# Rotary embedding on one core: VectorE one row ahead instead of two, the last rows without TensorE, and one semaphore less

## The chip, the cores and the metric

The kernel runs on one core of one Trainium2 chip. The metric is the device time of one execution in microseconds, the median of several. The profile's own clock runs from the first to the last instruction or landing, and is about 1.4 us shorter than the measured time (161.2 us in the profile of an execution of 162.6 us). Here a run counts as slow when it took over 1.5% more than the fastest of the same kernel.

## The reference

```python
# x: (16, 512, 1024) fp32, num_heads = 16, head_dim = 64; cos, sin: (512, 32)
x = x.reshape(batch, seq, num_heads, head_dim)
x1, x2 = x[..., :half_dim], x[..., half_dim:]
out = concatenate([x1 * cos - x2 * sin, x1 * sin + x2 * cos], axis=-1)   # fp32
```

33.5 MB come in and 33.5 MB go out. Each element takes two products and one sum.

## The kernel before

The 16 x 512 positions form 8 groups of 8 "rows". A row is a 128 x 1024 tile, a group 4 MB. SBUF and PSUM are the two memories on the chip in which the kernel keeps its tiles. The ring, a buffer in SBUF whose places are used again in turn, holds five groups. A semaphore is a counter that one engine or DMA raises and another engine waits for. For each row u:

- VectorE multiplies x by cos into one of three PSUM buffers, `t1_ps`.
- GpSimd multiplies the swapped halves of x by -sin and sin into one of six SBUF buffers, `t2_sb`. In row 3 of each group VectorE does this.
- The two are added, by VectorE (rows 0, 2, 4, 5, 7) or by TensorE with an identity matrix, after which ScalarE copies the sum out of PSUM (rows 1, 3, 6).
- When a whole group is added, ScalarE's queue issues its store. A load into a used place of the ring waits for the store of the group that was there. The first load and the last store are split into two halves of 2 MB.

```python
PE2 = [u % 8 in (1, 3, 6) for u in range(NU)]        # rows added by TensorE
V2 = [u % 8 == VROW for u in range(NU)]              # sine product by VectorE
NT1 = 3; NT2 = 6; LEAD = 2
# ... cut ...
            for u in range(NU):                      # on TensorE
                if not PE2[u]:
                    continue
                pe.wait_ge(sem_m, u + 1)
                if V2[u]:
                    pe.wait_ge(sem_d, n_dve[u])
                else:
                    pe.wait_ge(sem_p, n_pool[u])
# ... two matmuls with the identity, added to t1_ps ...
            def mul(u):                              # on VectorE
                # ... wait for the load when a new one begins ...
                if V2[u]:
                    wait_t2_free(ve, u)
                    ve.tensor_tensor(t2_sb[:, u % NT2, :, :, :], swapped(k), over_heads(s_ps), mult
                    ).then_inc(sem_d, 1)
                if u >= NT1:                         # the PSUM buffer of row u - 3 must be free
                    v = u - NT1
                    if PE2[v]:
                        ve.wait_ge(sem_a, n_pe[v])
                    else:
                        ve.wait_ge(sem_v, n_comb[v])
                ve.tensor_tensor(t1_ps[:, u % NT1, :] ..., x_sb[...], c_ps[...], mult).then_inc(sem_m, 1)

            def comb(u):
                ve.wait_ge(sem_m, u + 1)
                ve.wait_ge(sem_p, n_pool[u])
                ve.tensor_tensor(xs[:, k, :], t1_ps[...], t2_sb[...], add).then_inc(sem_v, 1)

            for u in range(NU + LEAD):
                if u < NU:
                    mul(u)
                if u >= LEAD and not PE2[u - LEAD]:
                    comb(u - LEAD)
```

## Time and profile before

| before | value |
|---|---|
| time, median of the first 3 runs | 162.17 us (162.09 to 162.74) |
| profiled span | 161.2 us |
| VectorE, GpSimd busy | 131.5, 130.2 us |
| moved by DMA | 67.39 MB |
| VectorE's longest waits | 9.3 us for ScalarE, in 6 places |

The view of the waits (engine, line, tile, what it waited for: total us, times, longest us) has for the kernel before:

```profile
DVE t_ps L247 <- ACT x_sb L161: 9.3, 6, 3.1
...
POOL t_sb L216 <- DMA x_sb<-in_x_dram: 7.5, 3, 3.5
```

And the chain that ended last, by line:

```profile
DVE x_sb L258 20%; PE t_ps L187 20%; DVE t_ps L247 15%; POOL t_sb L216 6%; ACT x_sb L161 5%; DMA stage<-in_sin_dram 4%; DVE t_sb L238 4%; SPq L142 0%; SPq L145 0%; ACT s_sb L154 0%; ACT s_sb L155 0%; DVEq L246 0%; DVEq L257 0%; DVEq L244 0%; POOLq L134 0%
```

Read alone, this chain says that compute sets the time, and it nearly leaves the DMA out. It follows the last instruction back, and the last instruction ends at 151.4 us. The program ends 9.8 us later, with a store.

### The profile page before, as it was taken

How to read it: one execution, taken by the hardware profiler on the slowest of the kernel's cores; microseconds unless marked ns; L12 is line 12 of the kernel's file. 1: busy time of each engine (PE TensorE's matmuls, PEld its weight loads, DVE VectorE, ACT ScalarE, POOL GpSimd, SP SyncE). 2: the span in 40 equal slices, each digit the busy share in tenths (PEclk: the TensorE clock that was granted, in tenths of full speed). 3: DMA queues.
4: the chain of work that ended last, by engine and by line, in shares of the span. 5: the costliest groups of instructions: out<-in, count | busy, mean ns of one | idle time of the engine just before them, and what ended most of it. 6: DMA issues, size and time to landing. Idle time of an engine off the chain costs nothing.

```text
span 161.2 us, 579 instructions
## 1 busy us (share of the span) xinstructions
PE 80.9 (50%) x102; PEld 24.8 (15%) x102; DVE 131.5 (82%) x116; ACT 26.6 (16%) x27; POOL 130.2 (81%) x62
## 2 busy tenths in 40 slices
PE   6002908249438434644844584494584483785000
PEld 1001302102202110120220121022022021211000
DVE  0079299998799999996999999996999899978500
ACT  3010221120221122202012202202202211211200
POOL 1049999999999999999999899973999659995000
PEclk9955796955585987655687659555558555558555
DMA  4999999999999999999999999999999999999995
GB/s 150 387 454 488 407 423 472 407 390 390 415 496 390 415 480 409 407 480 415 401 480 407 415 472 415 407 480 415 407 480 415 399 480 423 399 480 415 399 431 236
DMA packets 2882, 67.39 MB, mean 418 GB/s; under 512 B 320, under 2 KB 576, under 8 KB 576
## 3 DMA queue, kind: packets, MB, share of 16 engines
q1 hardware_dynamic: 1584, 33.82, 49.6%
q10 hardware_dynamic: 1296, 33.56, 48.3%
q14 instruction: 2, 0.02, 0.0%
HBM read 33.82 MB, written 33.55 MB: 418 GB/s over the span
## 4 chain that ended last, share of the span: by engine, by line
DVE 39%; PE 20%; issue 17%; POOL 6%; ACT 6%; DMA 4%; SPq 1%; DVEq 0%; POOLq 0%
DVE x_sb L258 20%; PE t_ps L187 20%; DVE t_ps L247 15%; POOL t_sb L216 6%; ACT x_sb L161 5%; DMA stage<-in_sin_dram 4%; DVE t_sb L238 4%; SPq L142 0%; SPq L145 0%; ACT s_sb L154 0%; ACT s_sb L155 0%; DVEq L246 0%; DVEq L257 0%; DVEq L244 0%; POOLq L134 0%
## 5 line engine op out<-in xcount | busy, mean ns | idle before, releaser
L216 POOL TENSOR_TENSOR t_sb<-x_sb,s_sb 128x1024 f32<-128x1024 f32 x56 | 129.5, 2369 | 16.2 <-ACT s_sb L155 8.8
L187 PE MATMUL t_ps<-t_sb,ident 128*128 128x512 f32 x96 | 78.2, 964 | 67.3 <-DVE t_ps L247 49.7
L247 DVE TENSOR_TENSOR t_ps<-x_sb,tab_ps 128x1024 f32<-128x1024 f32 x64 | 77.2, 1227 | 11.1 <-ACT x_sb L161 9.3
L258 DVE TENSOR_TENSOR x_sb<-t_ps,t_sb 128x1024 f32<-128x1024 f32 x40 | 48.6, 1218 | 0.0
L161 ACT ACTIVATE x_sb<-t_ps 128x1024 f32<-128x1024 f32 x24 | 24.6, 1024 | 115.9 <-PE t_ps L187 115.9
L187 PEld LDWEIGHTS t_ps<-t_sb,ident 128*128 128x128 f32 x96 | 24.0, 275 | 120.8 <-DVE t_ps L247 88.0
L238 DVE TENSOR_TENSOR t_sb<-x_sb,tab_ps 128x1024 f32<-128x1024 f32 x8 | 9.7, 1210 | 0.0
L225 DVE COPY tab_ps<-stage 128x256 f32<-128x256 f32 x1 | 0.4, 428 | 7.8 <-DMA stage<-in_cos_dram 7.8
L173 PE MATMUL t_ps<-zero 128*128 128x512 bf16 x6 | 2.7, 630 | 1.3 <-DVE zero L221 1.3
L154 ACT ACTIVATE s_sb<-stage 128x256 f32<-128x256 f32 x1 | 0.4, 416 | 7.2 <-DMA stage<-in_sin_dram 7.2
L154 ACT ACT_TABLE_LOAD x1 | 1.3, 1283 | 0.8 <-PEq L291 0.8
L173 PEld LDWEIGHTS t_ps<-zero 128*128 128x128 bf16 x6 | 0.7, 137 | 2.4 <-DVE zero L221 1.2
L221 DVE MEMSET zero<- 128x256 uint32 x1 | 0.3, 272 | 0.9 <-PEq L291 0.9
L198 POOL MEMSET ident<- 128x128 f32 x1 | 0.2, 204 | 0.3 <-POOLq L291 0.3
L155 ACT ACTIVATE s_sb<-stage 128x256 f32<-128x256 f32 x1 | 0.4, 399 | 0.0
L200 POOL TENSOR_SCALAR_AFFINE_SELECT ident<-ident 128x128 f32<-128x128 f32 x1 | 0.3, 292 | 0.1
L291 POOL MEMSET const-float32-0.0<- 128x1 f32 x1 | 0.1, 98 | 0.3 <-issue 0.3
L227 DVE TENSOR_SCALAR tab_ps<-stage 128x32 f32<-128x32 f32 x1 | 0.2, 195 | 0.0
L228 DVE COPY tab_ps<-stage 128x32 f32<-128x32 f32 x1 | 0.2, 184 | 0.0
L291 POOL MEMSET const-bfloat16-1.0<- 128x1 bf16 x1 | 0.1, 101 | 0.0
L291 POOL MEMSET const-uint8-127<- 128x1 uint8 x1 | 0.1, 101 | 0.0
L291 POOL MEMSET const-float32-1.0<- 128x1 f32 x1 | 0.1, 98 | 0.0
## 6 DMA issues: line engine op xcount, KB each, us to landing
x_sb<-in_x_dram SPq DMA_DIRECT2D x7, 4096.0 KB, 35.6
out_dram<-x_sb ACTq DMA_DIRECT2D x7, 4096.0 KB, 26.2
x_sb<-in_x_dram SPq DMA_DIRECT2D x2, 2048.0 KB, 9.6
out_dram<-x_sb ACTq DMA_DIRECT2D x2, 2048.0 KB, 10.2
stage<-in_cos_dram SPq DMA_DIRECT2D x1, 128.0 KB, 7.5
stage<-in_sin_dram SPq DMA_DIRECT2D x1, 128.0 KB, 7.2
```

Of the source, the lines that this page charges most:

```text
L154: ae.activation(s_sb[:, :, 0, :], sv, COPY, scale=-1.0)
L155: ae.activation(s_sb[:, :, 1, :], sv, COPY).then_inc(sem_s, 1)
L161: ae.activation(xs[:, k, :], t1_ps[:, u % NT1, :], COPY).then_inc(sem_a, 1)
L173: pe.matmul(t1_ps[:, k, b * BANK:(b + 1) * BANK], zero[:, 0:P], zero[:], start=True, stop=True).then_inc(sem_w, 1)
L187: ins = pe.matmul(t1_ps[:, u % NT1, b * BANK:(b + 1) * BANK], ident[:], t2[:, b * BANK:(b + 1) * BANK], start=False, stop=True, skip_group ...
L200: pl.affine_select(out=ident[:], in_=ident[:], compare_op=mybir.AluOpType.is_equal, fill=0.0, base=0, pattern=[[-1, P]], channel_multiplier=1,
L216: pl.tensor_tensor(t2_sb[:, u % NT2, :, :, :], swapped(k), over_heads(s_sb[:, r]), mult).then_inc(sem_p, 1)
L225: ve.tensor_copy(c_ps, cv)
L238: ve.tensor_tensor(t2_sb[:, u % NT2, :, :, :], swapped(k), over_heads(s_ps), mult).then_inc(sem_d, 1)
L247: ve.tensor_tensor(t1_ps[:, u % NT1, :].rearrange("p (h d) -> p h d", d=HALF), x_sb[:, k, :, :, :].rearrange("p h t d -> p (h t) d"), c_ps ...
L258: ve.tensor_tensor(xs[:, k, :], t1_ps[:, u % NT1, :], t2_sb[:, u % NT2, :, :, :].rearrange("p h t d -> p (h t d)"), add,).then_inc(sem_v, 1)
L291: nc = _bacc.Bacc("TRN2", target_bir_lowering=False, num_devices=1)
```

## The change

The intent: with a lead of two rows, VectorE's product u reuses the PSUM buffer that the sum just ahead of it has read, and must wait for that sum to finish. With a lead of one, that sum lies two instructions back. The last four rows are all added by VectorE, so that no detour over TensorE and ScalarE ends the kernel. The semaphore of VectorE's sine products goes: the cosine product of the same row comes after it in order and has a semaphore that TensorE waits for anyway.

```diff
-    PE2 = [u % 8 in (1, 3, 6) for u in range(NU)]
-    V2 = [u % 8 == VROW for u in range(NU)]
+    PE2 = [u < NU - R // 2 and u % 8 in (1, 3, 6) for u in range(NU)]
+    V2 = [u < NU - R // 2 and u % 8 == VROW for u in range(NU)]
...
-    LEAD = 2
+    LEAD = 1
...
-                if V2[u]:
-                    pe.wait_ge(sem_d, n_dve[u])
-                else:
+
+                if not V2[u]:
                     pe.wait_ge(sem_p, n_pool[u])
...
-                    ve.tensor_tensor(
-                        t2_sb[:, u % NT2, :, :, :], swapped(k), over_heads(s_ps), mult
-                    ).then_inc(sem_d, 1)
+                    ve.tensor_tensor(t2_sb[:, u % NT2, :, :, :], swapped(k), over_heads(s_ps), mult)
```

Of rows 60 to 63 only row 62 was on TensorE, so one sum moves to VectorE.

More of the change, by code (lines that the diff above doesn't have):

```diff
@@ L65, in bass_split_heads_rope_kernel @@
     n_pool = count([not v for v in V2])
-    n_dve = count(V2)
     n_pe = count(PE2)
@@ L95, in bass_split_heads_rope_kernel @@
         sem_p = stack.enter_context(nc.semaphore("pool"))
-        sem_d = stack.enter_context(nc.semaphore("dve2"))
         sem_m = stack.enter_context(nc.semaphore("mul"))
```

## The prediction

> **What bounds the kernel now.** I read the page first: engines, slices, DMA queues.
>
> ```profile
> PE 80.9 (50%) x102; PEld 24.8 (15%) x102; DVE 131.5 (82%) x116; ACT 26.6 (16%) x27; POOL 130.2 (81%) x62
> ...
> DMA  4999999999999999999999999999999999999995
> ...
> q1 hardware_dynamic: 1584, 33.82, 49.6%
> q10 hardware_dynamic: 1296, 33.56, 48.3%
> ...
> HBM read 33.82 MB, written 33.55 MB: 418 GB/s over the span
> ```
>
> VectorE and GpSimd are busy for 82% and 81%, which tempts one to call them the bound. But the two DMA queues add up to 49.6 + 48.3 = 97.9% of all 16 engines' span, and every slice but the first and the last is at 9. To see whether that busy share is work, not waiting, I cut the span in three windows (columns: window, length, then each engine's busy time and count, clock, DMA share, GB/s).
>
> ```profile
> 0.00:2.00 2.00, 0.75 (x2) 0.28 (x3) 0.27 (x1) 1.19 (x1) 0.70 (x6) 1.00 0.00 0
> 2.00:156.00 154.00, 80.17 (x101) 24.49 (x99) 131.28 (x115) 25.38 (x27) 129.54 (x56) 0.65 1.00 428
> 156.00:161.20 5.20, 0.00 (x0) 0.00 (x0) 0.00 (x0) 0.00 (x0) 0.00 (x0) 0.50 0.63 271
> ```
>
> For 154 us the DMA share is 1.00 at 428 GB/s, and no compute instruction runs in the last 5.2 us. A finer cut gives 432 GB/s from 4 to 33.6 us (loads alone) and 431 from 150 to 156 us (stores alone): the mix does not change the rate. So 67.39 MB / 428 GB/s = 157.5 us, plus 2.0 us before the first byte, plus about 1.2 us for the last landing (160 to 161.2 us moves 14 GB/s), makes 160.7 us of the 161.2.
>
> The chain of waits ends in VectorE, and its last piece is at 149.03 us. It follows instructions, and its end is not the end of the program. What comes after it is in the timeline (start, duration, engine, line, operation).
>
> ```profile
> 147.89 1.23 DVE L247 TENSOR_TENSOR t_ps<-x_sb,tab_ps 128x1024 f32<-128x1024 f32 x1
> 149.03 2.35 DVE L258 TENSOR_TENSOR x_sb<-t_ps,t_sb 128x1024 f32<-128x1024 f32 x2
> 149.50 1.02 ACT L161 ACTIVATE x_sb<-t_ps 128x1024 f32<-128x1024 f32 x1 [4.04 <-PE t_ps L187]
> 151.46 0.55 ACTq L165 DMA_DIRECT2D out_dram<-x_sb  x1
> ```
>
> ```profile
> out_dram<-x_sb ACTq DMA_DIRECT2D x2, 2048.0 KB, 10.2
> ```
>
> The last store (2 MB) is issued at 151.46 and lands 9.7 us later, the shortest of the nine stores' times by the view of that line: 161.14, the end. At 431 GB/s its bytes need 4.9 us. The other half-group store was issued at 145.50; the median of the two is 10.2 us, so it took about 10.7 and landed near 156.2. The last store therefore waited behind it: its first packet starts at 154.6, some 3.1 us after its issue. The first load of the program shows what an issue costs on an idle queue: issued at 0.80, first packet at 2.2, 1.4 us. So the last store could have come about 3.1 - 1.4 = 1.7 us later at no cost. The earlier stores have more room: they are issued near 31.6, 49.6, 66.0, 83.9, 100.5, 118.6 and 136.0, while the trace has the store ahead of each landing at (from the second on) 55.9, 75.8, 95.1, 114.5, 132.1 and 141.8.
>
> **What the Trainium skill says.** (1) "DMA: Bandwidth & Descriptors", section "Where 436 GB/s comes from", puts the fabric ceiling at 435 GB/s; the 428 to 432 here agree, and leave 1 to 2%. (2) The same page, "Issuing engines are not separate DMA queues": DMAs of all issuing engines run on the same 16 DMA engines and interleave. The trace agrees: loads and stores together make the same 420 to 440 GB/s as either alone, so issuing a store earlier only takes rate from a load. (3) "VectorE: DVE Perf Modes", "The DRAIN you can't avoid": eight copies with a semaphore after each took the same 13.88 us as with one at the end, so the semaphore costs nothing extra. The trace before has only products with semaphores; product to product starts 1.13 us apart, no visible extra. (4) "SBUF — State Buffer", "Who interferes with whom": a VectorE instruction with at most one SBUF input, outside the two-port modes, does not contend with GpSimd. VectorE's products and sums each take one input from PSUM, and GpSimd's 56 products average 2369 ns, so one sum more should not slow GpSimd.
>
> **The change, part by part.** *One row ahead.* The order of VectorE goes from product(u), sum(u-2) to product(u), sum(u-1). Before, product(u) needs the PSUM buffer of row u-3, which the sum just ahead of it frees:
>
> ```profile
> 134.70 1.22 DVE L258 TENSOR_TENSOR x_sb<-t_ps,t_sb 128x1024 f32<-128x1024 f32 x1
> 135.95 1.23 DVE L247 TENSOR_TENSOR t_ps<-x_sb,tab_ps 128x1024 f32<-128x1024 f32 x1
> 137.09 1.22 DVE L258 TENSOR_TENSOR x_sb<-t_ps,t_sb 128x1024 f32<-128x1024 f32 x1
> ```
>
> Sum to product is 1.25 us from start to start, product to sum 1.14. By the trace 30 such pairs lose 0.12 to 0.19 us each, about 4.0 us. Now that sum is two instructions back, and the loss goes. Further, rows 1, 3, 6 of eight go to TensorE and ScalarE. Between product 3 and product 6 VectorE had three instructions (4, sum 2, 5), 3.4 us, against TensorE's 3.8 plus ScalarE's 1.03; now it has four. The waits view gives VectorE on ScalarE 9.3 us in 6 waits, the longest 3.15 of them at the start, which stays (the first sine product of row 1 is ready only at 14.8). So up to 6.2 us goes. *Last four rows.* Only row 62 of rows 60 to 63 was on TensorE; VectorE gets one sum, +1.14 us, and the last rows lose a 3.8 + 1.03 us detour, which ended at 150.5, ahead of VectorE's 151.4. *Semaphore.* The eight sine products keep their time, 1.21 us; TensorE waits for the product that follows in order, as it did. Gain 0.
>
> VectorE's sum: -4.0 - 6.2 + 1.1 = about -9 us at most. On the path that sets the end: nothing, since no byte is removed and the DMA is full without a pause. Direct effect 0 us.
>
> **The tail, where it could still show.** A first store issued earlier starts sharing the DMA engines earlier, and the last load lands later. Placing the first group's instructions by hand with the durations above, store 1 could be issued near 28.8 instead of 31.6, so the last load near 131 + 2.8 = 133.7 at most. From that landing L (before: 130.9): GpSimd's seven products at 2.31 end at L + 16.3. VectorE: product 59 starts at L + 6.9, TensorE and ScalarE are through with row 59 at L + 13.35, product 62 starts at L + 13.4, then sum 61, product 63, sum 62 and sum 63 at 1.14 each: end L + 19.15. The last store is thus issued between 150.1 and 152.9, against a limit of 151.46 + 1.7 = 153.2. It still queues.
>
> **Rivals.** *VectorE is the bound* (82% busy, most of the chain): then 9 us less, about 153 us. Against it: 67 MB in 153 us, less the 3.2 us of start and end, would be 450 GB/s, above anything seen here over a long window. *GpSimd takes the wait over*: sum(u-1) needs the sine product u-1, now with one row less of slack, so VectorE could stall. GpSimd waits 7.5 us for loads and is one to four rows ahead of the sums late in the run, so this speaks against a long stall; and the stores have over 3 us of slack from row to row. If it cost VectorE 3 us in the last group, the end would move to some 163.5. *Starved tail*: the last load lands later and the last store misses the queue: 1 to 2 us, 163 to 164. *The early store reorders the DMA traffic*, with no change in bytes: within 0.5 us either way.
>
> **Range and chances.** Predicted 162.1 us, the median before of 162.17 (162.09 to 162.74) with no shift to speak of. Below 161.3 there is hardly anything: start plus bytes plus landing. Above, the starved tail: 163.0. So 161.5 to 163.0. Faster by over 2% (under 158.9) would need more than 435 GB/s: 1%. Slower by over 2% (over 165.4) needs a stall of 5 us in the last group: 2%. Within 2%: 97%.
>
> **What would show it.** Right: DMA share 1.00 and about 428 GB/s from 2 to 156 us; the queues' sum near 98%; sum-to-product distance on VectorE 1.14 instead of 1.25; waits of VectorE for ScalarE down to about 3 to 4 us, and new idle time of VectorE before products (for loads) or sums (for GpSimd); 41 sums, 92 fp32 matmuls; the last store issued at 150 to 153 us, landing over 8 us later. Wrong: a slice with a DMA digit below 9 in the middle; a last store issued after 153.5 that lands 7 us later (starved); GpSimd's products longer than 2.37 us; or a span below 159 us, which would mean that the rate is no ceiling.

## More of the kernel before

VectorE is never held up by a load. GpSimd is, in three places.

## The result, and the profile after

| | before | after |
|---|---|---|
| median, 6 runs each | 162.24 us (162.09 to 162.76) | 162.30 us (162.11 to 162.87) |
| ratio of the fast runs | | 1.000, 95% interval 0.998 to 1.002 |

A ratio here is the mean time of one kernel's fast runs over that of the other's of the same rounds, so not quite the ratio of the quoted medians. The kernel takes the same time.

The page of the kernel after: busy times, DMA digits and queues.

```profile
PE 72.2 (45%) x98; PEld 24.8 (15%) x98; DVE 130.0 (81%) x117; ACT 25.5 (16%) x26; POOL 130.3 (81%) x62
...
DMA  4999999999999999999999999999999999999996
...
q1 hardware_dynamic: 1584, 33.82, 49.7%
q10 hardware_dynamic: 1296, 33.56, 48.4%
```

The windows of the kernel after (window, length, busy time and count of each engine, clock, DMA share, GB/s):

```profile
2.00:156.00 154.00, 71.42 (x97) 24.51 (x95) 129.75 (x116) 24.35 (x26) 129.55 (x56) 0.72 1.00 428
156.00:161.20 5.20, 0.00 (x0) 0.00 (x0) 0.00 (x0) 0.00 (x0) 0.00 (x0) 0.50 0.68 290
```

The DMA side is as it was: full without a gap, 428 GB/s, 98.1% of the engines' span. Compute is not as it was. VectorE's instructions in the middle of the kernel after (start, duration, engine, line, operation), where L242 is the product and L253 the sum:

```profile
124.85 1.22 DVE L253 TENSOR_TENSOR x_sb<-t_ps,t_sb 128x1024 f32<-128x1024 f32 x1
125.98 1.22 DVE L242 TENSOR_TENSOR t_ps<-x_sb,tab_ps 128x1024 f32<-128x1024 f32 x1
127.11 1.22 DVE L253 TENSOR_TENSOR x_sb<-t_ps,t_sb 128x1024 f32<-128x1024 f32 x1
128.24 1.22 DVE L242 TENSOR_TENSOR t_ps<-x_sb,tab_ps 128x1024 f32<-128x1024 f32 x1
132.26 1.23 DVE L242 TENSOR_TENSOR t_ps<-x_sb,tab_ps 128x1024 f32<-128x1024 f32 x1 [2.80 <-DMA x_sb<-in_x_dram]
```

From a sum to the next product it is now 1.13 us, where it was 1.25. The last line shows where the time went: VectorE is through with its group and waits 2.80 us for the last load. The waits of the kernel after:

```profile
POOL t_sb L213 <- DMA x_sb<-in_x_dram: 8.8, 3, 3.2
...
DVE t_ps L242 <- DMA x_sb<-in_x_dram: 7.7, 3, 2.8
...
DVE t_ps L242 <- ACT x_sb L159: 3.9, 7, 1.4
...
DVE x_sb L253 <- POOL t_sb L213: 0.6, 1, 0.6
```

The wait for ScalarE fell from 9.3 to 3.9 us. In its place stand 7.7 us for loads, at the sixth, seventh and eighth group. The wait for GpSimd that the shorter lead could have brought is 0.6 us, once, at the start. The chain that ended last has turned round with it:

```profile
DMA x_sb<-in_x_dram 24%; DMA out_dram<-x_sb 20%; POOL t_sb L213 11%; PE t_ps L184 9%; DVE t_ps L242 6%; DVE x_sb L253 5%; DMA stage<-in_sin_dram 4%; ACT x_sb L159 3%; SPq L140 0%; SPq L143 0%; DVE t_sb L235 0%; ACT s_sb L152 0%; ACT s_sb L153 0%; ACTq L125 0%; POOLq L134 0%
```

Loads and stores, absent before, make 44% of it, with nothing changed in the DMA. As soon as VectorE was quick enough to wait for a load, the chain led there. Little is needed for such a turn. The kernel with the semaphore alone taken away (below) has a VectorE as slow as before, which waits for a load once, 0.4 us long; its chain by engine:

```profile
DMA 45%; DVE 23%; issue 9%; PE 9%; ACT 3%; POOL 3%; SPq 1%; DVEq 0%; ACTq 0%
```

So the shares of this chain do not measure what an engine costs. The end, in the timeline of the kernel after:

```profile
148.75 2.35 DVE L253 TENSOR_TENSOR x_sb<-t_ps,t_sb 128x1024 f32<-128x1024 f32 x2
151.18 0.55 ACTq L163 DMA_DIRECT2D out_dram<-x_sb  x1
```

The last store is issued at 151.18 and lands at 160.86, 9.7 us later, as before. It still stands in the queue.

### The profile page after: what moved, and what is told of

Its sections match the earlier page's. It is cut to its first block, busy times and chain, and to the rows that moved or that the text cites. A ratio compares the mean times of both kernels' runs of the same rounds, so it can differ in the third digit from the quotient of the medians.

```text
span 160.9 us, 563 instructions
## 1 busy us (share of the span) xinstructions
PE 72.2 (45%) x98; PEld 24.8 (15%) x98; DVE 130.0 (81%) x117; ACT 25.5 (16%) x26; POOL 130.3 (81%) x62
## 4 chain that ended last, share of the span: by engine, by line
DMA 48%; DVE 12%; POOL 11%; PE 9%; issue 9%; ACT 3%; SPq 1%; ACTq 0%; POOLq 0%
DMA x_sb<-in_x_dram 24%; DMA out_dram<-x_sb 20%; POOL t_sb L213 11%; PE t_ps L184 9%; DVE t_ps L242 6%; DVE x_sb L253 5%; DMA stage<-in_sin_dram 4%; ACT x_sb L159 3%; SPq L140 0%; SPq L143 0%; DVE t_sb L235 0%; ACT s_sb L152 0%; ACT s_sb L153 0%; ACTq L125 0%; POOLq L134 0%
## 5 line engine op out<-in xcount | busy, mean ns | idle before, releaser
L184 PE MATMUL t_ps<-t_sb,ident 128*128 128x512 f32 x92 | 69.4, 911 | 69.7 <-POOL t_sb L213 44.8
L242 DVE TENSOR_TENSOR t_ps<-x_sb,tab_ps 128x1024 f32<-128x1024 f32 x64 | 77.0, 1221 | 11.8 <-DMA x_sb<-in_x_dram 7.7
L253 DVE TENSOR_TENSOR x_sb<-t_ps,t_sb 128x1024 f32<-128x1024 f32 x41 | 49.8, 1216 | 0.6 <-POOL t_sb L213 0.6
L159 ACT ACTIVATE x_sb<-t_ps 128x1024 f32<-128x1024 f32 x23 | 23.5, 1023 | 110.6 <-PE t_ps L184 110.6
## 6 DMA issues: line engine op xcount, KB each, us to landing
out_dram<-x_sb ACTq DMA_DIRECT2D x2, 2048.0 KB, 10.7
```

The lines of the kernel that those rows point to most:

```text
L159: ae.activation(xs[:, k, :], t1_ps[:, u % NT1, :], COPY).then_inc(sem_a, 1)
L184: ins = pe.matmul(t1_ps[:, u % NT1, b * BANK:(b + 1) * BANK], ident[:], t2[:, b * BANK:(b + 1) * BANK], start=False, stop=True, skip_group ...
L242: ve.tensor_tensor(t1_ps[:, u % NT1, :].rearrange("p (h d) -> p h d", d=HALF), x_sb[:, k, :, :, :].rearrange("p h t d -> p (h t) d"), c_ps ...
L253: ve.tensor_tensor(xs[:, k, :], t1_ps[:, u % NT1, :], t2_sb[:, u % NT2, :, :, :].rearrange("p h t d -> p (h t d)"), add,).then_inc(sem_v, 1)
```

## The experiments

This table gathers, from the traces, the moments that the argument turns on (us from the start of the span; "landed" is the end of the last store).

| kernel | first store issued | last load landed | last store issued | landed |
|---|---|---|---|---|
| before | 31.64 | 130.87 | 151.46 | 161.14 |
| after | 29.09 | 132.24 | 151.18 | 160.86 |
| one row of lead alone | 29.33 | 131.49 | 149.44 | 160.78 |
| last rows alone | 31.75 | 129.05 | 153.49 | 160.47 |
| semaphore alone | 31.50 | 131.07 | 150.47 | 161.35 |
| no arithmetic | 14.18 | 146.65 | 147.26 | 160.34 |
| after, run again | 29.51 | 131.56 | 150.42 | 160.56 |
| after, seven extra products | 29.09 | 132.29 | 152.23 | 160.49 |
| after, eight extra, first run | 30.27 | 135.21 | 155.41 | 164.30 |
| after, eight extra, second run | 30.47 | 132.76 | 152.97 | 163.05 |
| after, last product six times more | 29.07 | 132.25 | 158.77 | 165.41 |

My theory is that the DMA engines, full from 2 us on, set the end, and that all of VectorE's gain lies under them. The first rival: VectorE is the bound, and gains and losses of the parts cancel. The second: compute slows the DMA.

### One row of lead alone (`lead_only`)

```diff
-    LEAD = 2
+    LEAD = 1
```

> One row of lead instead of two, nothing else changed. Theory (the DMA engines' 67.39 MB set the end): 162.2 us, ratio 1.00 within 0.3%; VectorE's sum-to-product distance 1.13 us instead of 1.25, its waits for ScalarE about 4 us instead of 9.3, waits for loads of about 8 us in three places, last store issued near 151.5, DMA share 1.00 from 2 to 156 us. Rival 1 (VectorE is the bound): 9 us less, 153. Rival 2 (the parts cancel: the lead gains some us and another part gives them back): faster by 2 us or more.

Measured: 162.14 us against 162.10, ratio 0.999 (0.997 to 1.001). The median distance from sum to product is 1.135 us against 1.253. VectorE waits 3.7 us for ScalarE and 6.9 us for loads. The last store is issued 2.1 us sooner than expected and lands at the same time. The one part that speeds VectorE up brings nothing by itself, so there is no gain for another part to cancel.

### The last rows alone (`tail_only`)

```diff
-    PE2 = [u % 8 in (1, 3, 6) for u in range(NU)]
-    V2 = [u % 8 == VROW for u in range(NU)]
+    PE2 = [u < NU - R // 2 and u % 8 in (1, 3, 6) for u in range(NU)]
+    V2 = [u < NU - R // 2 and u % 8 == VROW for u in range(NU)]
```

> Two rows of lead as before; only row 62 moves from TensorE to VectorE. Theory: 162.2 us, ratio 1.00 within 0.3%, since the last store is issued about one sum (1.14 us) later, near 152.6 instead of 151.46, still before the store ahead of it has left the queue. Rival (the parts cancel: the last rows on VectorE lose what the lead gains): about 1 us slower, 163.3, or more.

Measured: 162.60 us against 162.10, ratio 1.003 (1.000 to 1.006). The upper end of this interval does not exclude half a percent, but the trace gives no hint of a cause: the last store is issued at 153.49, 2.0 us later than before, and lands at 160.47, no later. But that trace is of the fastest of the six executions (162.06 us, against 163.42 for the slowest), so it cannot show what the slower ones did. The loss of 1 us that the rival expects lies just outside the interval; a loss of half that lies inside it.

### The semaphore alone (`sem_only`)

```diff
-                if V2[u]:
-                    pe.wait_ge(sem_d, n_dve[u])
-                else:
+                if not V2[u]:
                     pe.wait_ge(sem_p, n_pool[u])
...
-                    ).then_inc(sem_d, 1)
+                    )
```

> Only the semaphore of VectorE's eight sine products is taken away, and TensorE's wait for it. Theory: 162.2 us, ratio 1.00; sine product to product stays at 1.13 us from start to start as with the semaphore. Rival (an increment costs VectorE something): that distance shorter by 0.03 us or more.

Measured: 162.55 us against 162.10, ratio 1.002 (0.999 to 1.004). From a sine product to the product after it, in this kernel without the semaphore:

```profile
119.95 1.21 DVE L234 TENSOR_TENSOR t_sb<-x_sb,tab_ps 128x1024 f32<-128x1024 f32 x1
121.08 2.35 DVE L241 TENSOR_TENSOR t_ps<-x_sb,tab_ps 128x1024 f32<-128x1024 f32 x2
```

That is 1.13 us. In the kernel before, with the semaphore, all eight of these distances are 1.128 or 1.129 us. An increment on a VectorE instruction costs nothing that these traces can show.

### No arithmetic (`dma_only`, wrong result)

```diff
-            # ScalarE: tables, copies out of PSUM, stores when a group is added
+            for c, (g, r, n) in enumerate(stores):
+                for cl, (gl, rl, nl) in enumerate(loads):
+                    if gl == g:
+                        ae.wait_ge(sem_in[cl], 16)
+                ae.dma_start(part(ov, g, r, n), tile(g, r, n)).then_inc(...)
...
-        on_gpsimd(nc.gpsimd)
-        on_tensor(nc.tensor)
-        on_vector(nc.vector)
```

> Wrong result on purpose: the same loads and stores in the same order, with the same ring, but no arithmetic at all; each store waits only for its own load. Theory: the DMA alone takes nearly all of the time: 160.5 to 162.3 us, at 428 to 432 GB/s. Rival 1 (VectorE is the bound, the DMA is merely spread over its time): clearly shorter, under 155 us. Rival 2 (compute takes rate from the DMA through SBUF): 2% or more shorter, with more than 437 GB/s.

Measured: 161.91 us against 162.10, ratio 0.998 (0.996 to 1.000). Its windows (here only GpSimd's busy time, clock, DMA share, GB/s):

```profile
2.00:156.00 154.00, 0.00 (x0) 1.00 1.00 429
156.00:161.20 5.20, 0.00 (x0) 1.00 0.61 262
```

With all arithmetic gone the kernel is 0.2 us shorter by the medians, at most 0.4% by the interval. The first store leaves at 14 us instead of 31.6, and the end moves by 0.8 us in the traces. This refutes both rivals: neither VectorE nor interference from compute holds the kernel up. With these transfers, taking away all arithmetic gained about 0.2%, so a quicker VectorE cannot be expected to gain more.

### Less to move (`few_before`, `few_after`, wrong results on purpose)

The same edit in both kernels. Loads from the sixth group on bring one row of eight, each store writes one row. The arithmetic is whole.

```diff
+                m = 1 if g * R >= RING else n
-                sp.dma_start(tile(g, r, n), part(xv, g, r, n)).then_inc(sem_in[c], 16)
+                sp.dma_start(tile(g, r, m), part(xv, g, r, m)).then_inc(sem_in[c], 16)
...
-                ae.dma_start(part(ov, g, r, n), tile(g, r, n)).then_inc(
+                ae.dma_start(part(ov, g, r, 1), tile(g, r, 1)).then_inc(
```

> Wrong result on purpose: the kernel before, with its arithmetic whole, but with less to move: loads from the sixth group on bring one row of eight, stores write one row of their group or half-group. So the DMA is no bound and VectorE's own pace shows. Theory: VectorE's last sum ends at 151 us or a little sooner, as in the whole kernel, because it never waited for a load there; the last store of 0.5 MB lands some 4 us later: span about 154 to 156.

> Wrong result on purpose: the changed kernel with the same smaller transfers. Theory: the 7.7 us in which VectorE waits for loads in the whole kernel fall away, its last sum ends near 143 to 144 us, span about 147 to 148: 7 to 8 us, about 5%, less than the kernel before with the same transfers. So the change does speed VectorE up and the DMA hides it. Rival (the change speeds nothing up, its new waits for GpSimd eat what it frees): the same span as the kernel before with the same transfers, within 1 us.

Measured: 157.01 us and 146.81 us. One of the four runs of the kernel before was slow (158.60); by the fast runs alone the medians are 156.55 and 146.81 us and the means 156.67 and 146.71, so the change makes the kernel about 10 us faster when the DMA is out of the way, 6.4%. The last instructions in the timeline, first of the kernel before, then of the kernel after, both with less to move:

```profile
150.59 2.35 DVE L259 TENSOR_TENSOR x_sb<-t_ps,t_sb 128x1024 f32<-128x1024 f32 x2
153.02 0.55 ACTq L166 DMA_DIRECT2D out_dram<-x_sb  x1
```

```profile
139.82 2.35 DVE L254 TENSOR_TENSOR x_sb<-t_ps,t_sb 128x1024 f32<-128x1024 f32 x2
142.25 0.55 ACTq L164 DMA_DIRECT2D out_dram<-x_sb  x1
```

Here the end follows the last sum by 3.1 us. In these two, VectorE waits 10.7 and 3.0 us for ScalarE, a difference of 7.7 us. Add 4.0 us from the sum-to-product distance, take off 1.1 us for the extra sum and 0.6 us for the new wait for GpSimd: 10.0 us, against 10.8 between the two last sums. So the gain is real and accounted for within 1 us, and it is larger than the 7 to 8 us I expected. Part of the surprise is the kernel before: with less to move its last sum ended at 152.94, not at 151.38 as in the whole kernel and "a little sooner" as expected. Measured from the whole kernel, the last sum comes 9.2 us sooner. Two things are left open. The granted TensorE clock was 0.69 in the one trace and 0.73 in the other, and the mean matmul 990 and 923 ns; how much of the shorter wait for ScalarE comes from that was not separated. And in the changed kernel with less to move GpSimd runs from its first product to its last without a pause:

```profile
10.11 129.45 POOL L214 TENSOR_TENSOR t_sb<-x_sb,s_sb 128x1024 f32<-128x1024 f32 x56 [8.74 <-ACT s_sb L154]
```

It ends at 139.56, 2.6 us before VectorE. With the DMA out of the way GpSimd would thus be the next limit, and a still quicker VectorE would gain little.

### How late may the last store be (`late6`)

```diff
+                for i in range(6 if u == NU - 1 else 0):
+                    ve.tensor_tensor(t1_ps[...], x_sb[...], c_ps[...], mult).then_inc(sem_x, 1)
+                    ve.wait_ge(sem_x, i + 1)
                 ve.tensor_tensor(t1_ps[...], x_sb[...], c_ps[...], mult).then_inc(sem_m, 1)
```

> The changed kernel, result right, with the very last product repeated six more times at 1.25 us, so the last store is issued 7.5 us later, near 158.7. Theory: about 2 to 3 us of this are swallowed by the queue, the rest shows: the store lands 7 us after its issue, near 165.7 by the profile's clock, so about 167 us. If the end hung on VectorE's chain all along: 7.5 us slower, 169.8.

Measured: 166.55 us, 4.25 us above the changed kernel's 162.30, for a store issued 7.6 us later. So 3.3 us were swallowed. In the timeline of its ScalarE queue and the view of the store line:

```profile
158.77 0.55 ACTq L165 DMA_DIRECT2D out_dram<-x_sb  x1
```

```profile
DMA to landing us min/median/max: 6.6/25.8/35.7
```

Now the last store is the shortest of the nine: 6.6 us, against 9.7 when it stands in the queue. If a store of this size that does not queue takes 6.64 us, as here, the changed kernel's last store could be issued up to 160.86 - 6.64 = 154.2 us without moving the end. That is an estimate of 3.0 us of slack.

### Extra work for VectorE (`extra8`, `after_again`, `extra8_again`, `extra7`)

```diff
+                for i in range(1 if u % R == 5 else 0):
+                    spent[0] += 1
+                    ve.tensor_tensor(t1_ps[...], x_sb[...], c_ps[...], mult).then_inc(sem_x, 1)
+                    ve.wait_ge(sem_x, spent[0])
                 ve.tensor_tensor(t1_ps[...], x_sb[...], c_ps[...], mult).then_inc(sem_m, 1)
```

> The changed kernel, result right, with one product per group of eight rows done twice on VectorE, eight in all, each about 1.25 us: 10 us more work. Theory: VectorE had 7.7 us of waits for loads and its last group ends one product later, near 152.3; the last store still queues: 162.3 us, ratio 1.00 within 0.4%. Rival (VectorE is the bound): about 10 us slower, 172.

Measured: 166.05 us by the median of all six, of which two were slow (167.32 and 168.24); the fast ones have a median of 165.20 and a ratio of 1.018 (1.013 to 1.022): clear of noise. My expectation failed. Neither theory fits: 10 us more work cost 2.9 us (the 3.8 us in an expectation below took the slow runs in). The trace has VectorE waiting 1.9 us for a load even so, and the last load lands 3.0 us later than in the changed kernel. From 58 to 128 us the DMA moved 421 GB/s, where the changed kernel had 431, both at a DMA share of 1.00: a full share does not show a full rate. The last store is issued at 155.41, 1.2 us past the limit just found. Issued so late it could have landed at 162.05 on an empty queue; it landed at 164.30. So VectorE's last sum explains a part of this trace's loss, and not all of it. I ran the kernel again on another chip, with the changed kernel unaltered as a control beside it.

> The changed kernel unaltered, as a control beside the two that follow. Theory: ratio 1.00 within 0.3%, about 162.2 us. If it is 1 to 2% slower here, chips or hours differ and the slow result of the run with eight extra products was that.

Measured: 162.36 us against 162.15, ratio 1.002 (1.000 to 1.003). On that chip the changed kernel is as fast as ever.

> The kernel with eight extra products once more. It came out 3.8 us slower than the kernel before, not level, and its trace has the store packets slower between 58 and 128 us. If that was the hour or the chip: 162.3 us now. If it belongs to the kernel: 164.5 to 166 again, with the slowest DMA engine's landings later by 1 us or more per group from the sixth load on.

Measured: 164.71 us, ratio 1.020 (1.015 to 1.024), all six fast. The loss belongs to the kernel. In this trace it arises earlier. The semaphore of a transfer goes up 16 times as its parts land. The last part of the first store lands at 57.2 us, 2.1 us after the fifteenth; in the changed kernel it lands at 54.8, 1.0 us after the fifteenth. The last part of the next store is 2.5 us behind the fifteenth, and at the end two parts trail, the last at 163.05. Whether it is one and the same of the 16 DMA engines that trails, the landings do not say. The last store was issued at 152.97, inside the slack, and took 10.1 us to land, so it was queued: here the end did not hang on VectorE's last sum. What these two kernels have in common is a first store issued at 30.3 to 30.5 us. The kernels without the loss issue it at 29.1 to 29.5, at 31.5 to 31.8, or at 14.2. So I removed the extra product of the first group alone.

```diff
-                for i in range(1 if u % R == 5 else 0):
+                for i in range(1 if u % R == 5 and u > R else 0):
```

> The kernel with extra products, result right, but none in the first group: seven of 1.25 us, 8.8 us of VectorE work, while the first store is issued when the changed kernel issues it (29.1 us) and not at 30.3 to 30.5. Theory (VectorE has the room; the 2.5 to 4 us of the eight-product kernel came from the moment at which the first store joins the loads, where one DMA engine fell 2 us behind): ratio 1.00 within 0.4%, 162.3 us. Rival (the extra work in the later groups costs DMA time or delays the last stores): 164.5 us or more, as with eight.

Measured: 162.17 us against 162.32, ratio 1.000 (0.998 to 1.002). The loss is gone, with seven extra products left in. Its waits and its last store:

```profile
DVE t_ps L253 <- ACT x_sb L161: 3.5, 7, 1.4
...
DVE t_ps L253 <- DMA x_sb<-in_x_dram: 0.7, 1, 0.7
```

```profile
152.23 0.55 ACTq L165 DMA_DIRECT2D out_dram<-x_sb  x1
```

VectorE's wait for loads has shrunk from 7.7 us to 0.7: of the 8.8 us of work, 7.0 us went into it, 0.4 into the wait for ScalarE, and 1.05 us into the slack of the last store, 8.45 together. This is the clean form of the test that the run with eight extra products should have been: VectorE can be burdened with 5% of its span more without any cost that these runs show.

What is shown about the loss is that it goes away when the one extra product of the first group is taken out. That this works through the moment at which the first store joins the loads fits the times above, but is not shown: I did not shift that store by itself, and in the first of the two traces the loss spread over the middle of the run. A rival is untested: that eight products are too many, wherever they stand, since with seven only 0.7 us of VectorE's waits for loads was left. Seven products with the first group among them would have told. Why one part of a store trails the others stays open.

### Lost time without memory traffic (`pause8`)

```diff
+                for i in range(5 if u % R == 5 else 0):
+                    spent[0] += 1
+                    ve.tensor_copy(zero[:, 0:32], zero[:, 32:64]).then_inc(sem_x, 1)
+                    ve.wait_ge(sem_x, spent[0])
```

> The changed kernel, result right, with five short copies of 128x32 one after another instead of each extra product: VectorE loses about as much time, some 1 to 1.5 us per group, but reads and writes almost nothing. If lost VectorE time is what delays the DMA (through when the stores are issued, or through the last group): as slow as the kernel with eight extra products. If it is the memory traffic of the extra products: 162.3 us, ratio 1.00.

Measured: 195.81 us, ratio 1.207. This did not test what it was meant to test. The group of the copies and the DMA digits in its page:

```profile
DMA  5999999999999979999995999979202970079768
...
L246 DVE COPY zero<-zero 128x32 bf16<-128x32 bf16 x40 | 42.9, 1073 | 1.1
```

I had reckoned 0.2 to 0.3 us for a copy, and it took 1.07 us on average. This mean hides that copies come in different lengths (minimum, median and maximum in ns):

```profile
L246 DVE COPY zero<-zero x40: 174/450/2272, 21.1 to 179.3; 128x32 bf16<-128x32 bf16 x40
```

Two of its timeline rows tell why (start, duration of all five):

```profile
47.40 5.47 DVE L246 COPY zero<-zero 128x32 bf16<-128x32 bf16 x5
...
178.22 1.28 DVE L246 COPY zero<-zero 128x32 bf16<-128x32 bf16 x5
```

Five copies take 5.47 us in the middle of the run, with GpSimd at its products, and 1.28 us in the last group, where GpSimd's last one ends at 178.63. The Trainium skill, "SBUF — State Buffer", section "Who interferes with whom", says that a VectorE copy in a two-port mode and a GpSimd instruction exclude each other for the whole instruction, and whoever comes second waits. These numbers agree: the longest copy, 2.27 us, is nearly as long as a GpSimd product (2.33 to 2.37 us in this trace), and the shortest takes 0.17 us. In which mode the copies ran, no run shows. The run is useful in another way: it shows what this kernel looks like when VectorE is the bound. VectorE is never held up by a load, and the DMA digits fall to 0 in places.

## Why the prediction was right

- **The bound.** Predicted: start, bytes at 428 GB/s and landing make 160.7 us, and nothing in compute counts. The sum itself is no proof, since its rate was read from the same trace. The proof is the kernel without arithmetic: its span is 160.4 us, its time 161.91 us, 0.2 below the kernel before. One reading holds less widely than it sounds. In this trace the mix of loads and stores does not change the rate, but a full share alone does not fix it: the first run with eight extra products moved 421 GB/s for 70 us at a share of 1.00, the kernel after 431.
- **VectorE's gain.** Predicted at most 9 us, hidden. With less to move it is about 10 us. The step that was too small is the wait for ScalarE: up to 6.2 us in the prediction, 7.7 us where no load holds VectorE up. The prediction let the longest of these waits, 3.15 us at the start, stand as it was; in the kernel after the longest is 1.4 us. The 4.0 us of the sum-to-product distance held.
- **The tail, placed by hand.** First store 28.8 predicted, 29.1 measured. Last load at most 133.7 predicted, 132.2 measured. From that landing, product 62 at 13.4 us and the end at 19.15 predicted, 13.1 and 18.9 measured.
- **The room of the last store.** Predicted 1.7 us, from the issue cost of an idle queue. Estimated from the run with a late last store: 3.0 us. The step took the issue cost of the first load against the first packet of the last store. The likely reason for the difference is that the 16 engines do not run dry at one moment: the store ahead lands on them between 154.9 and 156.0 us in the trace of the changed kernel, and the end is set by the last of them. The last store of the run with the last rows alone, 2.0 us later than before and no slower to land, shows the same: the prediction's limit of 153.2 was too strict. It stood on the safe side.
- **The rivals.** The wait for GpSimd is 0.6 us, once. A starved tail did not come. The early store did reorder the traffic (the last load lands 1.4 us later), and the end stayed within 0.3 us by the profile.
- **The semaphore.** Predicted 0; the distance is 1.13 us with it and without it.

What the prediction did not foresee is that the order in which stores join loads may cost 2.5 to 3 us, if that is what slowed the kernel with eight extra products. Its rival of that name allowed 0.5 us. The change did not meet such a loss, but the range would have been too narrow if it had, and nothing in the prediction told that the first store at 29.1 us would be spared what came with one at 30.3: that part was luck.

## What to carry to other kernels

Read the chain of waits together with what runs after its last piece: a chain that ends in VectorE at 151 us says little of a program that ends with a store at 161. When the DMA share is 1.00 from the first byte to the last, the kernel with its arithmetic taken out gives the floor in one run, and here it left 0.2 us to gain. A faster engine then shows as a new wait for loads (7.7 us here), and the room that it has is found by giving it work until the time moves.

## What the Trainium skill lacked or had wrong

- "DMA: Bandwidth & Descriptors", "Where 436 GB/s comes from", says that for transfers between HBM and SBUF the HBM side, about 358 GB/s, binds. It states this without a condition, and it does not hold for this program, which runs on one core: 428 GB/s were sustained here for 154 us, close to the fabric ceiling of 435 that the section names. The same section's own 16 MB measurement of 425 GB/s agrees with this.
- "VectorE: DVE Perf Modes", "The DRAIN you can't avoid", and its rules advise to minimize the count of operations, not of semaphores. For increments this holds (1.128 us with and without). It lacks the cost of a wait on the instruction just ahead: 1.25 us from start to start instead of 1.135 us, so about 0.12 us for 23 such pairs of 128x1024 fp32 instructions and 0.19 us for seven more, 4.0 us in this kernel.
- "SBUF — State Buffer", "Who interferes with whom", names the blocking of VectorE copies and GpSimd. It gives no size for small copies: five of 128x32 bf16 took 5.47 us beside GpSimd's products, and 1.28 us where the last product ended 0.4 us after the first copy began.
- No page that I read has it that one more VectorE product early in a kernel bound by DMA can cost 2.5 us with the same bytes moved (164.71 us with it, 162.17 without).
